# Values times probabilities over four query blocks at once in heads 0 to 6, and the constants at the end of on-chip memory

## The chip, the cores and the metric

The kernel runs on one NeuronCore of a Trainium2 chip. The metric is the device time of one execution in microseconds (us); of several runs the median is taken. The engines are TensorE (PE in the profile, with its weight loads as PEld), VectorE (DVE), ScalarE (ACT), GpSimd (POOL) and SyncE (SP), which only issues transfers here.

## The reference

A two-layer encoder on one sequence of 1024 tokens with 1024 features, all in fp32. Layer 0 mixes tokens by latent attention (A), layer 1 by differential attention (B); both have 8 heads with values 128 wide. Queries go in blocks of 128, and a token sees the chunks of 64 up to its own, so query block i needs keys of blocks 0 to i only.

```python
# mixer A, one query block i
logits = einsum('bqhd,bkhd->bhqk', qn_b, k_nope) + einsum('bqhd,bkd->bhqk', qr_b, k_rope)
logits = where(_chunk_mask(i * Q_BLOCK, s), logits * scale, NEG_BIG)
p = softmax(logits, axis=-1)
o = einsum('bhqk,bkhd->bqhd', p, v)
# mixer B: two maps per head
p = softmax(einsum('bqhmd,bkhmd->bmhqk', q_b, k) * scale - slopes * dist, masked)
a = p[:, 0] - lam * p[:, 1]
o = einsum('bhqk,bkhe->bqhe', a, v)          # then RMSNorm per head
# each layer
x = layernorm(ALPHA * x + mixer(x) @ w_o)
x = layernorm(ALPHA * x + (silu(x @ w_gate) * (x @ w_up)) @ w_down)
```

The change touches the two products of probabilities and values.

## The kernel before, in words

Each matrix product is done in three matmuls on values split into a high part (fp32r) and the low rest: high by high, high by low, low by high. So nearly every operand passes through a copy on ACT that rounds it (the high part) and a subtraction on DVE or GpSimd (the low part).

The program goes in stages: projections of A, attention A, its output projection with layer norm, feed-forward layer 0, attention B, its output projection, feed-forward layer 1. Only the attentions change.

`attention` runs both. It lists blocks (h, i), head by head with query blocks 0 to 7, but the last head in the order 6, 7, 4, 5, 2, 3, 0, 1 (`LAST_ORDER`), because the output projection begins with query blocks 6 and 7. At block b it emits the scores of block b + 2 (`score`), the transposes of block b (`turn`), the work put at that slot by hand (`fill`: the projections of queries, keys and values of the next head, and in B the norms of the head before), and after every second block `mix`, the product with the values for that pair. The order of instructions on each engine is then drawn up by the framework's planner, which simulates the engines with a cost of its own; `tc.high_priority` moves a part ahead in its order (in B the turns by 60 places, in A by 0).

One block: `softmax_block` (L209) computes scores into a PSUM bank, DVE adds the bias and finds the extreme (L222), ACT takes the exponential (L227), and GpSimd and DVE normalise (L1188 in A; L1342 to L1344 in B). `transpose_block` (L234) then turns the block of probabilities, 128 keys at a time, through TensorE (L148) into a PSUM bank of up to four key blocks, and splits them pair of key blocks by pair: the copy on ACT (L250) and the subtraction on DVE (L251) write a tile `[P, 2, 256]`, two key blocks by the 256 queries of a pair of query blocks. `pv_group` (L253) multiplies, for each key block of the pair, values (the weights of the matmul) by these 256 columns, three matmuls each (L262); the last key block of a pair concerns its second query block only, so there the matmuls are 128 wide.

`mix_a` (L1194) copies the 256 columns out of PSUM on ACT (L1198) and stores them with one DMA on SP to `o_dr[0][g][h]`; `mix_b` (L1350) copies them on DVE (L1353) into a tile that holds two heads, and `norm_b` and `norm_b2` norm and store a head later. In A the result takes one of three PSUM banks (`ps_m`) that the projections use too, in B the one bank `o`.

The tiles of transposed probabilities lie in pools `ptp` with five buffers (A) or four (B) for each of high and low. Memory is given out from two ends, left and right. At the very left lies the buffer in which GpSimd's transfers (`nc.gpsimd.dma_start`) put their descriptors; then come the constants (identity for the transposes, ones, small columns). At the right end is a reserved strip, `edge`.

Of the kernel before, what the change touches and what calls it, by code (L numbers as in the profile page):

```python
# [16 lines left out]
P = 128  # L17
# [4 lines left out]
H = 8  # L22
# [20 lines left out]
def trunk(  # L43
# [35 lines left out]
    cp = ctx.enter_context(tc.tile_pool(name="cp", bufs=1))  # L79
    sp = ctx.enter_context(tc.tile_pool(name="sp", bufs=8))  # L80

    ident = cp.tile([P, P], F32, tag="ident", name="ident")
    ones = cp.tile([P, P], F32, tag="ones", name="ones")
    cst = cp.tile([P, 48], F32, tag="cst", name="cst")
    edge = ctx.enter_context(tc.tile_pool(name="edge", bufs=1, side="right"))
    edge.tile([P, 504], F32, tag="edge", name="edge")
# [147 lines left out]
    def transpose_block(ptp, pts, l, i, name):  # L234
        qc = (i % 2) * P
        for jq in range(i // 4 + 1):
            nj = min(4, i + 1 - 4 * jq)
            pt = ps_t(f"pt_{name}_{jq}")
            for jj in range(nj):
                j = 4 * jq + jj  # L240
                tr(pt[:, jj * P:(jj + 1) * P], l[:, j * P:(j + 1) * P])
            for jp in range(2 * jq, 2 * jq + (nj + 1) // 2):
                n = min(2, i + 1 - 2 * jp)
                if i % 2 == 0:
                    pts[jp] = tuple(
                        ptp.tile([P, 2, 256], F32R, tag=f"pt{c}", name=f"pt{c}_{name}_{jp}") for c in "hl"
                    )
                src = pt[:, (jp % 2) * 256:(jp % 2) * 256 + n * P].rearrange("p (j q) -> p j q", j=n)
                hv, lv = (t[:, :n, qc:qc + P] for t in pts[jp])
                ends["pth"] = A.copy(hv, src).ins  # L250
                ends["ptl"] = V.tensor_tensor(lv, src, f32(hv), ALU.subtract).ins  # L251

    def pv_group(pts, g, v_of, name):  # L253
        po = ps_o(f"o_{name}")
        nj = 2 * g + 2
        for j in range(nj):
            hi, lo = pts[j // 2]
            vh, vl = v_of(j)
            c = slice(P, 256) if j == nj - 1 else slice(0, 256)
            first, last = j == 0, j == nj - 1  # L260
            for a, b, st, sp_ in ((vh, hi, first, False), (vh, lo, False, False), (vl, hi, False, last)):
                T.matmul(po[:, c], a, b[:, j % 2, c], start=st, stop=sp_, skip_group_check=True)  # L262
        return po

    def attention(score, turn, mix, fill, la, hp):
# [7 lines left out]
        for b, (h, i) in enumerate(blocks):  # L273
            if b and i % 2 == 0:
                mix(blocks[b - 1][0], blocks[b - 1][1] // 2)
# [7 lines left out]
        mix(blocks[-1][0], blocks[-1][1] // 2)  # L283
# [821 lines left out]
    with ast as st:  # L1105
# [3 lines left out]
        ptp = st.enter_context(tc.tile_pool(name="a1p", bufs=5, side="right", reuse_waits="tile"))  # L1109
# [429 lines left out]
```

## Time and profile before

| | |
|---|---|
| Time, median of 3 runs | 2282.62 us (2281.2 to 2283.95) |
| Time of the profiled execution: span from the first to the last instruction | 2280.9 us |
| PE busy | 2242.7 us (98%), 11410 matmuls |
| DVE, ACT, POOL busy | 1555.2 (68%), 1015.4 (45%), 847.9 us (37%) |
| DMA | 288.28 MB, mean 126 GB/s |
| L262, values times probabilities | 160 matmuls of each of three passes in A, and in B |
| L250 and L251, splitting the transposed blocks | 160 each in A, and in B |
| L1198 (A) and L1353 (B), copying the results out | 32 each |

Busy time counts a matmul from its start to its modelled end, and successive ones overlap: a matmul of 128 by 256 lasts 283 ns in the rows, but the next one starts 0.12 us after it. In rows of the timeline the first number is the start in us from the span's start, the second the length. In grouped rows the count is followed by the busy time, the mean length in ns, and the idle time before them with what ended it.

### The profile page before, as it was taken

How to read it: one execution, taken by the hardware profiler on the slowest of the kernel's cores; microseconds unless marked ns; L12 is line 12 of the kernel's file. 1: busy time of each engine (PE TensorE's matmuls, PEld its weight loads, DVE VectorE, ACT ScalarE, POOL GpSimd, SP SyncE). 2: the span in 40 equal slices, each digit the busy share in tenths (PEclk: the TensorE clock that was granted, in tenths of full speed). 3: DMA queues.
4: the chain of work that ended last, by engine and by line, in shares of the span. 5: the costliest groups of instructions: out<-in, count | busy, mean ns of one | idle time of the engine just before them, and what ended most of it. 6: DMA issues, size and time to landing. Idle time of an engine off the chain costs nothing.

```text
span 2280.9 us, 31110 instructions
## 1 busy us (share of the span) xinstructions
PE 2242.7 (98%) x11410; PEld 1912.7 (84%) x11410; DVE 1555.2 (68%) x2848; ACT 1015.4 (45%) x2097; POOL 847.9 (37%) x676
## 2 busy tenths in 40 slices
PE   8999999999999999999999999999999999999998
PEld 8899998888888887888889898888778888887886
DVE  5676665686766658777576657576677666658778
ACT  4455564342333324445465655564432333324444
POOL 2232341114444445555432424321014444436561
PEclk9999999999999999999999999999999999999999
DMA  5010125334445428544311202054244232337443
GB/s 202 14 35 31 41 71 199 142 132 150 153 149 184 141 102 334 190 175 157 104 45 33 67 27 70 21 211 155 86 164 150 84 114 95 112 128 298 163 178 150
DMA packets 105545, 288.28 MB, mean 126 GB/s; under 512 B 7968, under 2 KB 30112, under 8 KB 94896
## 3 DMA queue, kind: packets, MB, share of 16 engines
q1 hardware_dynamic: 100976, 275.87, 34.1%
q0 software_dynamic: 4416, 10.42, 1.7%
q8 instruction: 90, 1.47, 0.3%
q14 instruction: 63, 0.52, 0.1%
HBM read 205.00 MB, written 77.07 MB: 124 GB/s over the span
## 4 chain that ended last, share of the span: by engine, by line
PE 92%; DVE 3%; DMA 2%; issue 1%; ACT 1%; POOL 0%; SPq 0%; DVEq 0%; POOLq 0%; ACTq 0%
PE gb L549 15%; PE gc L549 10%; PE ga L549 10%; PE dw L830 7%; PE dx L830 5%; PE s_a L219 4%; PE zp_a L417 3%; PE s_b L219 3%; PE dv L830 3%; PE dy L830 3%; PE bp L145 3%; PE bp L143 3%; PE bp L144 3%; PE o_a L262 2%; PE o_b L262 2%; PE hq L1038 1%
## 5 line engine op out<-in xcount | busy, mean ns | idle before, releaser
L503 ACT CAST op_g<-gr 128x512 fp32r<-128x512 f32 x240 | 146.8, 621 | 369.3 <-PE gb L549 180.2
L504 POOL TENSOR_TENSOR op_g<-gr,op_g 128x512 fp32r<-128x512 f32 x104 | 145.2, 1401 | 250.1 <-ACT op_g L503 144.5
L504 DVE TENSOR_TENSOR op_h<-rh,op_h 128x512 fp32r<-128x512 f32 x154 | 158.6, 1057 | 62.1 <-ACT op_h L503 62.1
L549 PE MATMUL ga<-xh_m,op_g 128*128 128x512 f32 x512 | 168.2, 389 | 0.0
L503 ACT CAST op_h<-rh 128x512 fp32r<-128x512 f32 x154 | 92.9, 619 | 138.4 <-PE dx L830 36.5
L830 PE MATMUL dw<-op_w_t,op_h 128*128 128x512 f32 x660 | 151.2, 390 | 0.0
L830 PEld LDWEIGHTS dw<-op_w_t,op_h 128*128 128x128 f32 x660 | 123.6, 188 | 25.7 <-DVE op_h L504 0.2
L227 ACT ACTIVATE l_b<-l_b,mx_b 128x256 f32<-128x256 f32 (+7 forms) x128 | 99.4, 777 | 76.8 <-DVE mx_b L222 72.8
L1343 POOL TENSOR_SCALAR l_b<-l_b,rb,cst 128x128 f32<-128x128 f32 (+3 forms) x64 | 52.5, 821 | 205.1 <-DVE rb L1342 193.6
L830 PE MATMUL dx<-op_w_b,op_h 128*128 128x512 f32 x528 | 123.1, 394 | 5.4 <-ACT op_w_b L503 3.9
L504 POOL TENSOR_TENSOR op_w_t<-tt,op_w_t 128x512 fp32r<-128x512 f32 x66 | 99.4, 1510 | 76.0 <-ACT op_w_t L503 74.7
L830 PEld LDWEIGHTS dx<-op_w_b,op_h 128*128 128x128 f32 x528 | 99.9, 190 | 28.4 <-ACT op_w_b L503 4.7
L504 DVE TENSOR_TENSOR op_g<-gr,op_g 128x512 fp32r<-128x512 f32 x136 | 110.7, 820 | 14.3 <-ACT op_g L503 14.0
L549 PE MATMUL gb<-t4h_f,op_g 128*128 128x512 f32 x352 | 115.9, 390 | 3.3 <-DVE tmp L632 3.3
L504 POOL TENSOR_TENSOR op_g<-s,op_g 128x512 fp32r<-128x512 f32 x40 | 55.5, 1388 | 168.8 <-ACT op_g L503 160.6
L549 PE MATMUL gb<-t3h_f,op_g 128*128 128x512 f32 x352 | 115.5, 389 | 2.0 <-DVE tmp L628 2.0
L549 PE MATMUL gb<-t2h_f,op_g 128*128 128x512 f32 x352 | 115.6, 390 | 0.4 <-DVE op_g L504 0.4
L549 PE MATMUL gc<-t1h_f,op_g 128*128 128x512 f32 x352 | 115.6, 389 | 0.1
L549 PE MATMUL gc<-b22h_f,op_g 128*128 128x512 f32 x352 | 115.3, 389 | 0.0
L549 PEld LDWEIGHTS ga<-xh_m,op_g 128*128 128x128 f32 x512 | 96.1, 188 | 19.9
L143 PE MATMUL bp<-xT_f,h_wb 128*128 128x512 f32 x256 | 101.7, 397 | 0.0
L144 PE MATMUL bp<-xT_f,h_wb 128*128 128x512 f32 x256 | 101.5, 397 | 0.0
(384 smaller groups left out, 6718.9 us busy)
## 6 DMA issues: line engine op xcount, KB each, us to landing
gr<-in_w_gu SPq DMA_DIRECT2D x44, 1024.0 KB, 7.0
rh<-h_dr SPq DMA_DIRECT2D x28, 1024.0 KB, 6.3
h_dr<-sh SPq DMA_DIRECT2D x22, 1024.0 KB, 4.9
h_dr<-hp SPq DMA_DIRECT2D x22, 768.0 KB, 4.1
tt<-in_w_dn SPq DMA_DIRECT2D x22, 512.0 KB, 7.8
rh<-h_dr SPq DMA_DIRECT2D x14, 768.0 KB, 4.3
wo_dr<-op_pwo SPq DMA_DIRECT2D x16, 512.0 KB, 3.5
z<-xs_dr SPq DMA_DIRECT2D x16, 512.0 KB, 10.1
```

The source lines that it names most:

```text
L143: T.matmul(ps_out, lh, rh, start=(i == 0), stop=False)
L144: T.matmul(ps_out, lh, rl, start=False, stop=False)
L145: T.matmul(ps_out, ll, rh, start=False, stop=(i == n - 1))
L219: T.matmul(s[:, :w], lh, rh[:, ks], start=(j == 0), stop=(j == len(q_pass) - 1))
L227: ends["exp"] = A.activation(l[:, :n], l[:, :n], AF.Exp, bias=mx, scale=-1.0, accum_out=sm).ins
L262: T.matmul(po[:, c], a, b[:, j % 2, c], start=st, stop=sp_, skip_group_check=True)
L417: T.matmul(m, a[:, h, :], self.wo[h][w][:, c], start=(start and h == heads[0] and a is oh and w == 0), stop=(stop and h == heads[-1] and a ...
L503: A.copy(hi, src)
L504: return eng.tensor_tensor(lo, src, f32(hi), ALU.subtract).ins
L549: T.matmul(o, w[:, a, kc], x[b][:, k, :], start=(first and k == 0 and (a, b) == (0, 0)), stop=(k == 3 and a == 1), skip_group_check=True,)
L830: T.matmul(o, h[:, a, c], w[:, b_], start=(first and (a, b_) == (0, 0)), stop=(last and a == 1), skip_group_check=True,).ins for a, b_ in ...
L1343: G.tensor_scalar(l1[:, :n], l1[:, :n], r[:, 1:2], nlam, ALU.mult, ALU.mult)
```

## The change

- In heads 0 to 6 of both attentions a mix covers four query blocks instead of two (`wide(h)` is 4); head 7 stays at two. Its matmuls are 512 wide, and 384, 256 and 128 wide for the last three key blocks. A PSUM bank of results holds 512 columns.
- The transposed probabilities lie in tiles of 2048 columns: four key blocks by four query blocks, or for head 7 all eight key blocks by two. One copy and one subtraction split a whole bank of up to four key blocks, in all heads. There are two such tiles for each of high and low.
- `mix_a` copies 512 columns out and issues two DMAs, `mix_b` copies 512 columns.
- The constants move to the right end; `edge` shrinks so that the right end is filled as far as before. The descriptor buffer of GpSimd's transfers shrinks from the default (16384 bytes per partition) to 1024, and a pad keeps the left side at a distance of exactly 16 KB from its old place.

```diff
-    cp = ctx.enter_context(tc.tile_pool(name="cp", bufs=1))
+    cp = ctx.enter_context(tc.tile_pool(name="cp", bufs=1, side="right"))
+    cst = cp.tile([P, 48], F32, tag="cst", name="cst")
+    ones = cp.tile([P, P], F32, tag="ones", name="ones")
+    ident = cp.tile([P, P], F32, tag="ident", name="ident")
+    cp.tile([P, 200], F32, tag="edge", name="edge")
     sp = ctx.enter_context(tc.tile_pool(name="sp", bufs=8))
...
-    edge.tile([P, 504], F32, tag="edge", name="edge")
+    base = ctx.enter_context(tc.tile_pool(name="base", bufs=1))
+    base.tile([P, 48], F32, tag="pad", name="pad")
...
+    def wide(h):
+        return 4 if h < H - 1 else 2
...
-            for jp in range(2 * jq, 2 * jq + (nj + 1) // 2):
-                n = min(2, i + 1 - 2 * jp)
-                if i % 2 == 0:
-                    pts[jp] = tuple(
-                        ptp.tile([P, 2, 256], F32R, tag=f"pt{c}", name=f"pt{c}_{name}_{jp}") for c in "hl"
-                    )
-                src = pt[:, (jp % 2) * 256:(jp % 2) * 256 + n * P].rearrange("p (j q) -> p j q", j=n)
-                hv, lv = (t[:, :n, qc:qc + P] for t in pts[jp])
-                ends["pth"] = A.copy(hv, src).ins
-                ends["ptl"] = V.tensor_tensor(lv, src, f32(hv), ALU.subtract).ins
+            k = jq if n == 4 else 0
+            if k not in pts:
+                pts[k] = tuple(
+                    ptp.tile([P, 2048], F32R, tag=f"pt{c}", name=f"pt{c}_{name}_{jq}") for c in "hl"
+                )
+            src = pt[:, :nj * P].rearrange("p (j q) -> p j q", j=nj)
+            hv, lv = (
+                t.rearrange("p (j c q) -> p j c q", c=n, q=P)[:, 4 * (jq - k):4 * (jq - k) + nj, q]
+                for t in pts[k]
+            )
+            ends["pth"] = A.copy(hv, src).ins
+            ends["ptl"] = V.tensor_tensor(lv, src, f32(hv), ALU.subtract).ins
...
-        nj = 2 * g + 2
+        n = wide(h)
+        nj = n * g + n
         for j in range(nj):
-            hi, lo = pts[j // 2]
+            hi, lo = pts[j // 4 if n == 4 else 0]
             vh, vl = v_of(j)
-            c = slice(P, 256) if j == nj - 1 else slice(0, 256)
+            q0 = max(0, j - n * g) * P
+            at = (j % 4 if n == 4 else j) * n * P
...
-                T.matmul(po[:, c], a, b[:, j % 2, c], start=st, stop=sp_, skip_group_check=True)
+                T.matmul(po[:, q0:n * P], a, b[:, at + q0:at + n * P], start=st, stop=sp_, skip_group_check=True)
...
-            if b and i % 2 == 0:
-                mix(blocks[b - 1][0], blocks[b - 1][1] // 2)
+            if b:
+                hp_, ip = blocks[b - 1]
+                if ip % wide(hp_) == wide(hp_) - 1:
+                    mix(hp_, ip // wide(hp_))
...
-        ptp = st.enter_context(tc.tile_pool(name="a1p", bufs=5, side="right", reuse_waits="tile"))
+        ptp = st.enter_context(tc.tile_pool(name="a1p", bufs=2, side="right", reuse_waits="tile"))
...
-            ob = vp.tile([P, 256], F32, tag="ob", name=f"ob{h}_{g}", bufs=2)
-            A.copy(ob, po[:, :256])
-            nc.sync.dma_start(o_dr[0][g][h], ob)
+            n = wide(h) // 2
+            ob = vp.tile([P, 512], F32, tag="ob", name=f"ob{h}_{g}", bufs=2)[:, :n * 256]
+            A.copy(ob, po[:, :n * 256])
+            for k in range(n):
+                nc.sync.dma_start(o_dr[0][n * g + k][h], ob[:, k * 256:(k + 1) * 256])
...
-        ptp = st.enter_context(tc.tile_pool(name="b1p", bufs=4, reuse_waits="tile"))
+        ptp = st.enter_context(tc.tile_pool(name="b1p", bufs=2, reuse_waits="tile"))
...
-            V.tensor_copy(o_rows(h, g), po[:, :256])
+            n = wide(h) // 2
+            V.tensor_copy(o_rows(h, n * g, n), po[:, :n * 256])
...
-    nc = bacc.Bacc("TRN2", target_bir_lowering=False, num_devices=1)
+    nc = bacc.Bacc("TRN2", target_bir_lowering=False, num_devices=1, dynamic_dma_scratch_size=1024)
```

21 lines of the change are left out of this document (9 added, 12 removed).

## The prediction

> **What bounds the kernel now.** I read the per-core line and the page first, then the chain that ended last, then the two attention stages by stretches, then who made TensorE wait in them, and last the single matmuls in order of time, because the change touches one matmul loop and what feeds it.
>
> ```profile
> core 0: 2280.9 us, clock 0.997
> PE 2242.7 (98%) x11410; PEld 1912.7 (84%) x11410; DVE 1555.2 (68%) x2848; ACT 1015.4 (45%) x2097; POOL 847.9 (37%) x676
> PE 92%; DVE 3%; DMA 2%; issue 1%; ACT 1%; POOL 0%; SPq 0%; DVEq 0%; POOLq 0%; ACTq 0%
> ```
>
> TensorE is busy 98% of the span at full clock and is 92% of the chain. The two attentions lie at about 95 to 355 us (A) and 1130 to 1550 us (B). Stretches of them (columns: stretch, its length, then busy us of PE, its weight loads, DVE, ACT, POOL; granted clock; DMA share; GB/s):
>
> ```profile
> 150.00:200.00 50.00, 50.00 (x338) 46.30 (x337) 33.05 (x99) 29.66 (x81) 16.04 (x18) 1.00 0.12 38
> 250.00:300.00 50.00, 50.00 (x330) 45.91 (x329) 36.09 (x102) 29.10 (x80) 12.65 (x15) 1.00 0.08 25
> 1200.00:1300.00 100.00, 100.00 (x628) 89.52 (x627) 68.52 (x195) 60.26 (x142) 32.95 (x31) 1.00 0.15 43
> 1500.00:1560.00 60.00, 57.65 (x319) 47.70 (x318) 45.16 (x123) 36.04 (x89) 15.42 (x17) 1.00 0.49 189
> ```
>
> TensorE is full in them, VectorE at 66 to 75%, ScalarE at about 60%, GpSimd at about 30%. Only the tail of B (head 7) has gaps. The waits of TensorE confirm it: between 95 and 360 us the view lists none, and between 1130 and 1560 us only these three.
>
> ```profile
> PE zp_a L417 <- DMA wo<-wo_dr: 1.3, 1, 1.3
> PE s_b L219 <- DVE bk L1327: 1.3, 1, 1.3
> PE pt_b L148 <- DVE l_b L1344: 0.8, 2, 0.7
> ```
>
> So inside heads 0 to 6 a microsecond less of TensorE work is a microsecond less of time, as long as no new wait appears, and work saved on ACT or DVE is worth nothing by itself.
>
> **What a matmul costs.** The length of a matmul in the rows overlaps its successor; what counts is the distance from one start to the next. Starts in us, then the modelled length; the last fence is a piece of the chain.
>
> ```profile
> 142.97 0.28 PE L262 MATMUL o_a<-ptl_a,vh 128*128 128x256 f32 x1
> 143.09 0.28 PE L262 MATMUL o_a<-pth_a,vl 128*128 128x256 f32 x1
> 143.21 0.22 PE L262 MATMUL o_a<-pth_a,vh 128*128 128x128 f32 x1
> 143.27 0.28 PE L262 MATMUL o_a<-ptl_a,vh 128*128 128x128 f32 x1
> 143.38 0.27 PE L262 MATMUL o_a<-pth_a,vl 128*128 128x128 f32 x1
> 143.49 0.48 PE L219 MATMUL s_a<-kn,qh 128*128 128x512 f32 x1
> ...
> 158.27 0.34 PE L219 MATMUL s_a<-kn,ql 128*128 128x384 f32 x1
> 158.45 0.34 PE L219 MATMUL s_a<-ck_hi,qr 128*128 128x384 f32 x1
> 158.63 0.27 PE L148 MATMUL pt_a<-ident,l_a 128*128 128x128 f32 x1
> ```
> ```profile
> 226.78 2.81 PE o_a L262 x24
> ...
> 501.78 2.72 PE gb L549 x12
> ```
>
> The three 128-wide matmuls that close a group take 143.49 - 143.21 = 0.28 us together. The 24 of a whole group of pair 3 take 2.81, so its 21 256-wide ones take (2.81 - 0.28) / 21 = 0.1205 each. 512-wide ones with a new weight each take 2.72 / 12 = 0.2267 (the FFN row), 384-wide ones 0.18. Two 256s (0.241) thus cost 0.014 more than one 512: every matmul carries some 13 ns beside its columns, and a 128-wide one does not fall to half of a 256.
>
> **The change, part by part.** (1) The mix over four query blocks. Per head of 0 to 6 and attention the old loop issues, for groups of 2, 4, 6 and 8 key blocks, 3 x (1+3+5+7) = 48 matmuls of 256 and 12 of 128: 48 x 0.1205 + 4 x 0.28 = 5.78 + 1.12 = 6.90 us. The new one has two groups, of 4 and 8 key blocks, in which the last four narrow from 512 to 128: 18 of 512, 6 of 384, 6 of 256, 6 of 128. That is 18 x 0.2267 + 6 x 0.18 + 6 x 0.1205 + 2 x 0.28 = 4.08 + 1.08 + 0.72 + 0.56 = 6.44 us. The columns are the same (4608 x 3); 24 matmuls fewer per head save 0.46 us, and 14 heads save 6.4 us. The 384 row is read to 0.01 us only, which leaves 84 x 0.005 = 0.4 us either way. Head 7 keeps pairs.
>
> On this the Trainium skill says otherwise ("TensorE: Matmul & The Clock Gate", Back-to-back issue gap): columns over 2.4 GHz plus about 2.5 ns for a warm matmul by itself. By that an old head would take 5.91 us and a new one 5.85, and the sum would be 0.8 us instead of 6.4. The rows show about 13 ns where the page has 2.5, with a weight load before every matmul, and 0.28 for three 128s where it gives 0.17; the same section does warn that a stream of loads and matmuls is spaced by both. I take the rows.
>
> (2) Splitting the transposed probabilities: one copy (ACT) and one subtraction (DVE) per bank of up to four key blocks instead of one per pair, in all heads.
>
> ```profile
> L250 ACT CAST pth_a<-pt_a 128x256 fp32r<-128x256 f32 x128 | 45.3, 373 | 25.3 <-PE pt_a L148 14.5 <-DVE ptl_a L251 9.1 <-PE s_a L219 0.4
> L250 ACT CAST pth_a<-pt_a 128x128 fp32r<-128x128 f32 x32 | 8.6, 269 | 7.7 <-DVE ptl_a L251 4.1 <-PE pt_a L148 3.5
> L251 DVE TENSOR_TENSOR ptl_a<-pt_a,pth_a 128x256 fp32r<-128x256 f32 x128 | 51.7, 420 | 13.9 <-ACT pth_a L250 12.7
> L251 DVE TENSOR_TENSOR ptl_a<-pt_a,pth_a 128x128 fp32r<-128x128 f32 x32 | 9.2, 286 | 1.8 <-ACT pth_a L250 1.7
> L1198 ACT COPY ob<-o_a 128x256 f32<-128x256 f32 x32 | 12.0, 375 | 17.9 <-PE o_a L262 10.2 <-issue 6.7 <-DMA o_dr<-ob 0.6
> L1353 DVE COPY bo<-o_b 128x256 f32<-128x256 f32 x32 | 13.5, 421 | 14.0 <-PE o_b L262 13.9
> ```
>
> By the slope from 128 to 256 a 512-wide copy is about 373 + 2 x 104 = 0.58 us on ACT and 420 + 2 x 134 = 0.69 on DVE; the constant is 0.17 and 0.15. A head goes from 20 of each to 12, so 8 x 0.17 = 1.3 us of ACT and 1.2 of DVE go per head, some 20 us of each over 16 heads. Both are covered by a full TensorE: zero. If the cover were gone, they would be a gain. Against them stands a later hand-over: the first matmul of a key quad waits for 0.58 + 0.69 instead of 0.37 + 0.42, about 0.5 us.
>
> (3) The copies out (L1198, L1353) go from four to two per head, each twice as wide; zero on the path by the same cover. The DMAs to o_dr stay 32 and of the same size, issued in twos on SP up to two blocks later; SP has the next head's weights queued behind them, which are asked for a head ahead. Their reader, the output projection, begins with the last head, which is not regrouped. Zero.
>
> (4) Buffers of the transposed probabilities: two wide ones per half (2 x 8 KB) instead of five (A) or four (B) of 2 KB. A second group needs both, so the copy for its second key quad (block 4) waits until the mix over blocks 0 to 3 has read its tile, and the next head's block 0 until the first half of the mix over blocks 4 to 7 is done. Queued behind that copy on ACT are the exponentials of the blocks two ahead, and on them DVE, GpSimd and the next transposes. The new mixes are also longer at a time, 1.9 and 4.6 us. The trace has no such wait, so I bound it: from below zero, since five and four buffers already go round within one head (the last pair takes four) and TensorE shows no wait from it in A; the nearest rows are what the weight loads of the mix wait for now.
>
> ```profile
>   DVE ptl_b L251: 0.4, 1
>   ACT pth_a L250: 0.4, 1
>   DVE ptl_a L251: 0.3, 1
>   ACT pth_b L250: 0.3, 1
> ```
>
> From above it is 0.4 at each of the 28 mixes, 11.2 us. I take zero, since four such waits in 64 mixes is nearer to none, and TensorE has projections and scores of later blocks to run meanwhile.
>
> (5) The identity, ones and small constants at the other end of memory, everything on the left 16 KB lower. No row shows a cost by address: the transposes that read the identity are 0.27 us against scores of every tile. Zero; a nanosecond either way on some 750 transposes bounds it at 0.8 us.
>
> (6) A descriptor buffer of 1 KB instead of the default 16 KB for transfers issued by GpSimd.
>
> ```profile
> q0 software_dynamic: 4416, 10.42, 1.7%
> L1320 POOL DMA_DIRECT2D bq<-bq x32 | 17.7, 553 | 36.1 <-ACT bq L1316 35.8
> bq<-bq POOLq DMA_DIRECT2D x32, 128.0 KB, 2.7
> ```
>
> 4416 packets in all; in B 32 small transfers, landing 2.7 us after issue. If each had to wait for its forerunner to land, GpSimd would stand 32 x 2.7 = 86 us in B with the normalisation of the probabilities queued behind, which is the upper end; the lower is zero, which I take, since the transfers come in twos, several us apart. The Trainium skill ("DMA: Bandwidth & Descriptors", Terms and The descriptor swizzle) gives 16 bytes per descriptor and 9 per engine for a 128-partition transfer; an estimate from it is 64 descriptors, seven transfers at once. No run here shows the limit.
>
> **The sum.** -6.4 + 0. The profiled span is 2280.9, the median of the runs 2282.6, 1.7 us above it; off the median the forecast is 2276.2.
>
> **The rivals.**
> - Stalls at the group edges (slower). Place: the first block of each group, point (4). Break-even is 6.4 / 28 = 0.23 us per mix; at the 0.4 of the wait rows the loss is 11.2 and the time 2282.6 - 6.4 + 11.2 = 2287.4. For it: in B the turns are put 60 places ahead, so the copies run ahead into the buffer wait, and ACT is in order. Against it: TensorE has run 260 us in A without a listed wait at 60% ACT.
> - Half of that, or a TensorE that starves for some microseconds in blocks 4 to 7 because the work of a mix has moved to later blocks: about 2281, no change that can be told.
> - The change doesn't do what it says: the 13 ns belong to the columns and only the page's gap goes. By rows, with 0.2267 / 512 per column for all wide ones and 0.28 for the closing three, 3.1 us go: 2279.5, within the measurement. (By the Trainium skill's gap it would be 0.8 us, 2281.8.)
> - More than the sum: the fewer ACT and DVE instructions also close B's tail, where TensorE is idle 2.35 of 60 us and the three listed waits add to 3.4: 2282.6 - 6.4 - 3.4 = 2272.8.
> - GpSimd's buffer blocks: B stretched by up to 86 us; anything over 6.4 us loses.
>
> **How the numbers follow.** About 0.2% (4.6 us) is what a measurement of this kernel can tell from no change; the runs spread over 2.8 us. Forecast (stalls under 1.8 us in sum) 0.50, more than the sum 0.10: faster 0.60. Half-stalls 0.19, columns only 0.05: same 0.24. Stalls at the edges 0.13, GpSimd's buffer 0.03: slower 0.16. The range runs from 2271 (the tail's gain and a low run) to 2286 (most of the stalls), and leaves out the buffer and the worst stalls. The likeliest case alone is 2274 to 2278.
>
> **What the profile after would show.** L262 with 104 matmuls per pass and attention (7 x 12 + 20) instead of 160, and a chain piece of 24 of them of about 4.6 us; L250 and L251 96 times each per attention; L1198 and L1353 18 times. A's stage some 3.2 us shorter, B's the same, the FFN stages as before. PE waits at ACT or DVE still near none in A: if rows such as o_a behind pth_a, or pt behind l, appear with several us, step (4) was wrong. If L1320 lasts longer than 0.55 us, step (6) was. If starts of 512-wide mix matmuls lie more than 0.227 apart without a wait, step (1) was. What most easily makes the forecast wrong is the order of instructions, which the planner draws up anew for the whole program.

## The result and the profile after

The changed kernel takes 2297.63 us in the median (2296.65 to 2297.93, 5 runs) against 2282.71 (2281.2 to 2283.95, 5 runs) of the kernel before on the same chip: ratio 1.0064, 95% interval 1.0052 to 1.0077. It is 14.9 us slower; the forecast was 2276.2, with a range up to 2286. The profiled execution spans 14.0 us more than before. From its page, the per-core line, the busy times and the shares of the chain:

```profile
core 0: 2294.9 us, clock 0.997
PE 2245.1 (98%) x11074; PEld 1895.9 (83%) x11074; DVE 1543.5 (67%) x2706; ACT 999.3 (44%) x1955; POOL 842.9 (37%) x676
PE 85%; DVE 7%; DMA 3%; issue 2%; ACT 2%; POOL 1%; SPq 0%; DVEq 0%; POOLq 0%; ACTq 0%
```

TensorE issues 336 matmuls fewer and is busy 2.4 us longer in a longer span; its share of the chain that ended last fell from 92 to 85%, and VectorE's rose from 3 to 7. The same stretches as before (columns as there):

```profile
150.00:200.00 50.00, 46.68 (x266) 40.41 (x265) 30.58 (x84) 26.91 (x60) 15.68 (x17) 1.00 0.11 34
250.00:300.00 50.00, 46.34 (x265) 39.58 (x264) 34.24 (x88) 25.89 (x58) 12.55 (x14) 1.00 0.09 27
1200.00:1300.00 100.00, 97.23 (x565) 85.19 (x564) 64.18 (x173) 56.78 (x122) 32.83 (x28) 0.98 0.16 48
1500.00:1560.00 60.00, 56.83 (x312) 48.69 (x311) 46.68 (x114) 35.66 (x77) 13.53 (x16) 0.97 0.58 215
```

In the stretches of A, where TensorE was full, 3.3 and 3.7 of 50 us are now empty, while ACT and DVE have less to do than before. What TensorE waits for, first in A (95 to 370 us), then in B (1120 to 1590 us; total us, times, longest; `s` are scores, `mx` the extreme that L222 finds, `o` the results of a mix, `pth` the high part of the transposed probabilities; line numbers shift by a few from kernel to kernel):

```profile
PE s_a L219 <- DVE mx_a L222: 7.4, 9, 1.9
PE o_a L271 <- ACT pth_a L257: 1.1, 2, 0.9
PE v L143 <- DVE kn L1188: 0.7, 2, 0.4
```
```profile
PE s_b L219 <- DVE bk L1340: 3.2, 2, 2.4
PE s_b L219 <- DVE mx_b L222: 2.2, 3, 1.4
PE pt_b L148 <- DVE l_b L1357: 0.8, 1, 0.8
```

A had no such line before. The largest entry is not at the mix: it is a score matmul (L219) that waits until DVE has emptied a bank of scores (L222). Copies of 512 columns last what was estimated (0.58); these groups, and where A begins and ends (the last numbers of the last two rows are the first and the last start in us):

```profile
L257 ACT CAST pth_a<-pt_a 128x512 fp32r<-128x512 f32 x48 | 27.5, 584 | 13.6 <-PE pt_a L148 13.2
L1210 ACT COPY ob<-o_a 128x512 f32<-128x512 f32 x14 | 8.2, 586 | 15.6 <-PE o_a L271 15.6
L219 PE MATMUL s_a<-kn,qh x192: 220/367/504, 83.8 to 351.3; 128*128 128x384 f32 x48, 128*128 128x512 f32 x48, 128*128 128x320 f32 x32, 128*128 128x448 f32 x32
L271 PE MATMUL o_a<-pth_a,vl x104: 272/336/398, 107.5 to 358.5; 128*128 128x512 f32 x42, 128*128 128x256 f32 x30, 128*128 128x128 f32 x18, 128*128 128x384 f32 x14
```

From the first score to the last matmul of the mix A takes 358.5 - 83.8 = 274.7 us; the same two rows of before give 347.9 - 84.3 = 263.6. Stages measured in this way are what the experiments below are read by (B from its first score to its last mix matmul; the way out of A up to the first matmul of feed-forward layer 0, FFN for short; layer 1 from its first matmul to the last instruction):

| profiled execution, us | A | A's last mix to the FFN | B | FFN layer 1 | span |
|---|---|---|---|---|---|
| before | 263.6 | 93.4 | 418.4 | 654.4 | 2280.9 |
| after | 274.7 | 94.1 | 421.6 | 653.4 | 2294.9 |
| e1_pairs | 265.2 | 94.1 | 429.2 | 652.3 | 2287.9 |
| e2_no_buffer_wait | 274.4 | 100.2 | 426.8 | 651.1 | 2303.6 |
| e3_memory | 264.1 | 93.4 | 418.1 | 653.6 | 2280.5 |
| e5_first_wide / e6_second_wide | 266.7 / 269.6 | 103.5 / 101.9 | 422.6 / 430.6 | 651.6 / 653.1 | 2297.8 / 2307.1 |
| e9_deferred_pairs / e12_tied_pairs | 264.0 / 268.7 | 103.2 / 101.2 | 430.1 / 429.6 | 654.2 / 652.4 | 2297.9 / 2296.9 |
| e14_held_projections | 262.9 | 100.2 | 426.6 | 654.4 | 2295.3 |
| e16_more_out_buffers | 262.9 | 94.5 | 424.3 | 652.2 | 2286.0 |
| e17_wide_in_a | 263.0 | 94.3 | 418.3 | 649.6 | 2278.8 |
| e19_pairs_held | 268.1 | 93.4 | 418.4 | 652.6 | 2284.3 |

Of the 14.0 us, 11.1 are A's and 3.2 B's. From first score to last mix matmul TensorE is empty for 9.7 us of A, 0.2 before. In B, before and after:

```profile
1130.80:1549.16 418.36, 414.75 (x2522) 366.97 (x2521) 286.32 (x803) 248.06 (x576) 135.12 (x129) 1.00 0.22 71
1142.56:1564.17 421.61, 415.16 (x2354) 360.98 (x2353) 276.99 (x725) 242.39 (x515) 134.85 (x130) 0.99 0.23 71
```

TensorE is empty for 3.6 us of B before and 6.5 after. Twice in the changed B, from 1239.0 and from 1515.5 us, its clock is at half for 3.4 us, and TensorE is full in both stretches, so some 3.4 us of work are lost there; in B of before this does not happen. So B has 2.8 us more of empty time, 3.4 us of slow clock and about 3 us less of work, and is 3.2 us longer.

One change of heads in A shows how it comes about. Matmuls of the changed kernel in order of time, then VectorE at the same time (start, length; in brackets idle time and what ended it):

```profile
153.22 0.39 PE L143 MATMUL kn<-ck_hi,h_wa 128*128 128x512 f32 x1
...
153.68 0.40 PE L145 MATMUL kn<-ck_hi,l_wa 128*128 128x512 f32 x1
153.91 0.33 PE L219 MATMUL s_a<-kn,qh 128*128 128x128 f32 x2
...
155.25 0.28 PE L219 MATMUL s_a<-ck_lo,qr 128*128 128x256 f32 x1
157.39 0.62 PE L219 MATMUL s_a<-kn,qh 128*128 128x384 f32 x2 [1.86 <-DVE mx_a L222]
...
160.12 1.15 PE L148 MATMUL pt_a<-ident,l_a 128*128 128x128 f32 x9
...
164.75 0.39 PE L271 MATMUL o_a<-ptl_a,vh 128*128 128x512 f32 x1
164.98 0.40 PE L271 MATMUL o_a<-pth_a,vl 128*128 128x512 f32 x1
```
```profile
153.42 2.79 DVE L1138 TENSOR_TENSOR qrb<-qr,sin 32x512 f32<-32x512 f32 x4
156.43 0.69 DVE L258 TENSOR_TENSOR ptl_a<-pt_a,pth_a 128x512 fp32r<-128x512 f32 x1
157.04 0.28 DVE L222 CUSTOM_DVE_ANT_0 l_a<-s_a,ba 128x128 f32<-128x128 f32 x1
```

The projection of the next head's keys (kn) has its last matmul at 153.68. Then TensorE has only scores of the next head's first blocks left, and a few transposes. They need a bank each, there are two, and DVE, which frees them, is at the rotary part of the queries for 2.79 us. From 155.5 to 157.39 TensorE stands; after the rotary part, DVE first splits a bank of transposed probabilities (0.69 us). The transposes of the old head's block 7 begin at 160.12. Of the mix over blocks 4 to 7 one matmul runs at 162.25 and the others from 164.75, 0.23 us from start to start, as computed. In the kernel before, the mix of blocks 4 and 5 did not depend on block 7, and at the same change of heads it fills the place after the next head's first score. These are the first and the last of its matmuls from 149.96 on:

```profile
149.96 0.34 PE L262 MATMUL o_a<-ptl_a,vh 128*128 128x256 f32 x1
...
152.07 0.28 PE L262 MATMUL o_a<-pth_a,vl 128*128 128x128 f32 x1
```

### The profile page after: what moved, and what is told of

It reads as the page before. It is cut to its first block, busy times and chain, and to the rows that moved or that the text cites. A ratio compares the mean times of both kernels' runs of the same rounds, so it can differ in the third digit from the quotient of the medians.

```text
span 2294.9 us, 30116 instructions
## 1 busy us (share of the span) xinstructions
PE 2245.1 (98%) x11074; PEld 1895.9 (83%) x11074; DVE 1543.5 (67%) x2706; ACT 999.3 (44%) x1955; POOL 842.9 (37%) x676
## 4 chain that ended last, share of the span: by engine, by line
PE 85%; DVE 7%; DMA 3%; issue 2%; ACT 2%; POOL 1%; SPq 0%; DVEq 0%; POOLq 0%; ACTq 0%
PE gb L560 15%; PE gc L560 10%; PE ga L560 10%; PE dw L841 6%; PE zp_a L428 3%; PE s_b L219 3%; PE s_a L219 3%; PE dv L841 3%; PE bp L143 3%; PE bp L144 3%; PE bp L145 3%; PE dy L841 2%; PE o_b L271 2%; PE o_a L271 2%; DVE tt L803 1%
## 5 line engine op out<-in xcount | busy, mean ns | idle before, releaser
L515 POOL TENSOR_TENSOR op_g<-s,op_g 128x512 fp32r<-128x512 f32 x40 | 54.3, 1356 | 166.7 <-ACT op_g L514 110.3
L143 PE MATMUL bp<-xT_f,h_wb 128*128 128x512 f32 x256 | 101.9, 398 | 0.1
L145 PE MATMUL bp<-xT_f,l_wb 128*128 128x512 f32 x256 | 101.4, 396 | 0.0
## 6 DMA issues: line engine op xcount, KB each, us to landing
z<-xs_dr SPq DMA_DIRECT2D x16, 512.0 KB, 10.3
```

Source lines behind the costliest of these rows:

```text
L143: T.matmul(ps_out, lh, rh, start=(i == 0), stop=False)
L145: T.matmul(ps_out, ll, rh, start=False, stop=(i == n - 1))
L515: return eng.tensor_tensor(lo, src, f32(hi), ALU.subtract).ins
```

## The experiments

Five theories stood at the start. *Lumps*: the wide mix has its data only when the last of four blocks is transposed, so TensorE has no independent work at the change of heads. *Buffers*: the copy of transposed probabilities waits on ACT for one of two wide tiles, and the softmax queues behind it (point (4) of the prediction). *Copies*: one copy per bank hands over later. *Memory*: the moved constants or the small descriptor buffer. *Order*: the planner's new order is worse by chance. The code excerpts show only the lines that matter. All times are medians, with the ratio to the kernel before on the same chip and its 95% interval.

**e3_memory: the memory part alone** (attentions as before; constants, pad and 1 KB buffer as after).

```diff
+    cp = ctx.enter_context(tc.tile_pool(name="cp", bufs=1, side="right"))
...
+    nc = bacc.Bacc("TRN2", target_bir_lowering=False, num_devices=1, dynamic_dma_scratch_size=1024)
```

> The kernel before, with only the constants at the right end, the pad, and the descriptor buffer of 1 KB. Theory memory: 2290 or more. Theories buffers, lumps, order: 2281 to 2284, the stages as before to 0.5 us, and GpSimd's transfers still issued in 0.55 us.

2281.91 us, 0.9997 (0.9988 to 1.0007). No stage moves by more than 0.8 us. The queries' small transfers on GpSimd take as long as before (553 ns there), with a landing time of 3.0 us (2.9 before in the same stretch, 1120 to 1560 us):

```profile
L1320 POOL DMA_DIRECT2D bq<-bq x32 | 17.7, 555 | 36.6 <-ACT bq L1316 36.0 <-issue 0.5
bq<-bq POOLq DMA_DIRECT2D x30, 128.0 KB, 3.0
```

*Memory* falls.

**e1_pairs: pairs in all heads, the rest as after.**

```diff
     def wide(h):
-        return 4 if h < H - 1 else 2
+        return 2
```

> The changed kernel, but with the mix over two query blocks in all heads again; the constants' place, the small descriptor buffer, the single copy per bank and the two 8 KB tiles stay. Theory buffers (two tiles make the copies on ACT wait for the mix) and theory lumps (TensorE lacks the mix of the first pair as reserve work in blocks 4 to 7): both are gone with pairs, so the time is that of before, 2281 to 2284 us, attention A again 264 us from its first score to the first output projection matmul instead of 275. Theory memory (places or the descriptor buffer): stays near 2297. Theory order (the planner's new order is bad by chance): anywhere from 2278 to 2300, A and B moving independently.

2289.96 us, 1.0038 (1.0023 to 1.0052). A is back at 265.2: of the 11.1 us, 9.5 come and go with the wide mix, and 1.6 stay with e1. The time misses the 2281 to 2284 because of B: 429.2, with its loss at the end (head 7), where TensorE waits 4.1 us at once for a normalised block. Part of that figure is a shifted border. In e1 21 matmuls of the output projection, which came after the last mix, run before it, and the way from B to feed-forward layer 1 is 4.8 us shorter (72.6 instead of 77.4; 70.8 to 71.4 in e9, e11 and e12 below). Both together are 501.8 us in e1, 495.7 in the kernel before.

**e2_no_buffer_wait: a third tile for the probabilities in A** (13 instead of 16 blocks of columns in the tile that holds the triangle; one `ob` buffer pays for it).

```diff
+                d = tri and (jq == i // 4 if n == 4 else i // 2 in (1, 2))
-                    ptp.tile([P, 2048], F32R, tag=f"pt{c}", name=f"pt{c}_{name}_{jq}") for c in "hl"
+                    ptp.tile([P, (13 if d else 16) * P], F32R, tag=f"pt{c}{'d' if d else ''}",
+                             name=f"pt{c}_{name}_{jq}", bufs=(2 if d else 1) if tri else 2) for c in "hl"
...
-            ob = vp.tile([P, 512], F32, tag="ob", name=f"ob{h}_{g}", bufs=2)[:, :n * 256]
+            ob = vp.tile([P, 512], F32, tag="ob", name=f"ob{h}_{g}", bufs=1)[:, :n * 256]
```

> The changed kernel, but in A the tiles of transposed probabilities no longer wait for a mix: two tiles of 13 blocks for the diagonal quads and one of 16 for the full quad, for each of high and low; one buffer instead of two for the copied result pays for it. B as changed. Theory buffers: the ACT waits for the mix (12.0 us in five in A) go, and A falls from 275 to 261 to 264 us, the time to 2283 to 2287. Theory lumps: the waits at ACT go, A stays over 270, the time over 2292. Theory order: A anywhere, with other places of waiting.

2306.3 us, 1.0106 (1.0091 to 1.0121). Of the 8.7 us that its span has over the changed kernel's, 6.2 lie in the way out of A, where copies into the single `ob` wait 5.4 us for stores, and 5.2 in B, whose instructions are the same. The wait it is aimed at is there in the changed kernel, in ACT's waits from 95 to 362 us:

```profile
ACT pth_a L257 <- PE o_a L271: 12.0, 5, 3.6
```

In e2 ACT has no such wait in A any more, yet A takes 274.4 and TensorE waits for mx_a 7.7 us. In A, *buffers* names a real wait that isn't on the path. For B no run takes it away (9.6 us in eight waits in the changed kernel).

**e5_first_wide and e6_second_wide: only blocks 0 to 3, or only 4 to 7, in one mix.**

```diff
-    def wide(h):
-        return 4 if h < H - 1 else 2
+    def span(h, i):
+        return (0, 4) if h < H - 1 and i < 4 else (i - i % 2, 2)      # e5
+        return (4, 4) if h < H - 1 and i > 3 else (i - i % 2, 2)      # e6
```

> The changed kernel with the four-block mix only for query blocks 0 to 3 of heads 0 to 6; blocks 4 to 7 go in pairs, so that the mix of blocks 4 and 5 (2 us of TensorE) is there to run while blocks 6 and 7 are on their way. Theory lumps: A comes back to 262 to 266 us, nearly all of the 11 lost. Theory order: A has no reason to differ from the changed kernel's 275, or lands anywhere.

> The reverse: the four-block mix only for blocks 4 to 7, pairs for blocks 0 to 3. Theory lumps: the loss stays, A 270 to 276 us, TensorE waiting for score banks around the change of heads. Theory order: anywhere.

2298.89 us, 1.0069 (1.0054 to 1.0084), and 2312.55, 1.0131 (1.0115 to 1.0146). A takes 266.7 and 269.6: 1.5 and 4.4 over e1, both together 9.5. Each lies just outside what *lumps* asked for, 262 to 266 and 270 to 276. The mix over blocks 4 to 7 carries more, and TensorE's waits for score banks are none in e5 and 4.4 us in e6. In both, the way out of A is longer too: TensorE waits 7.5 and 6.4 us at once for the last copy into `ob` (7.8 and 6.1 in e9 and e12 below), which lies on ACT behind copies of the output projection's input that wait for their transfer.

**e4_rope, e7_later_projections, e8_three_ahead: more work near the gap by the order of the program.** e4 puts the rotary part of the queries two slots earlier, e7 the projections of the second half one slot later, e8 scores three blocks ahead with three banks (and one bank less for the transposes).

```diff
-                at(b + 7, q_rope, h // 2, 1)
+                at(b + 5, q_rope, h // 2, 1)                          # e4
-            at(b + (6 if h < H - 1 else 4), q_nope, h, 1)
-            at(b + (7 if h < H - 1 else 5), k_nope, h, 1)
+            at(b + (7 if h < H - 1 else 4), q_nope, h, 1)             # e7
+            at(b + (8 if h < H - 1 else 5), k_nope, h, 1)
-PS_BUFS_A = (2, 3, 3)
+PS_BUFS_A = (3, 3, 2)                                                 # e8
...
-        attention(score_a, turn_a, mix_a, fill, 2, (0, 0))
+        attention(score_a, turn_a, mix_a, fill, 3, (0, 0))            # e8
```

> The changed kernel, with the second half of the rotary queries (five DVE operations in a row, 3.5 us) put two slots earlier, from block 7 to block 5 of the head before. Theory lumps: the two places where TensorE waits 2.0 + 0.5 + 0.3 us for a score bank while DVE works on them go, A falls by 4 to 8 us, the time to 2290 to 2294. Theory buffers: the same waits for the mix stay and A stays at 273 to 276, the time at 2296 to 2298. Theory order: A anywhere.

> The changed kernel with the second halves of the query and key projections in A (2.0 and 1.4 us of TensorE) one slot later, in block 7 and in block 0 of the next head instead of blocks 6 and 7, so that TensorE has independent work at the change of heads. Theory lumps: the waits for score banks there fall by half or more, A to 263 to 270. Theory order: A 271 to 278 with other places of waiting.

> The changed kernel with the scores of A three blocks ahead instead of two, three score banks instead of two (two instead of three for the transposes) and five tiles of probabilities instead of four; the first and the last head's key projections a slot earlier, as the scores need them. Theory lumps: TensorE can run the next head's first scores while block 7 is on its way, the waits for score banks (7.4 us in nine) go, A 260 to 268. If the score banks are only where a shortage elsewhere shows (DVE), A stays over 270.

2303.12 us, 1.0092 (1.0077 to 1.0107); 2302.85, 1.0095 (1.0079 to 1.011); 2314.39, 1.0134 (1.0117 to 1.0151). A stays at 274.9, 275.5 and 277.3, and *lumps* misses all three. In e4 the rotary part no longer stands in the gaps (the one at the change of heads shown is 1.36 us instead of 1.86), but the waits for score banks still sum to 7.7 us. In e8 they fall to 1.5, and TensorE is empty elsewhere instead, 10.5 us of A in all against 9.7. So neither the rotary part on DVE nor the number of score banks is the cause by itself. The place in the program decides little, since the planner draws up its own order.

**e10_reserve: the mix over blocks 0 to 3 emitted after block 6.**

```diff
+                if late and wide(hp_) == 4:
+                    if ip in (6, 7):
+                        mix(hp_, ip - 6)
```

> The changed kernel with the tiles of the run e2_no_buffer_wait in A, the results copied out 256 columns at a time from two buffers as before, and in A, heads 0 to 6, the mix of blocks 0 to 3 held back to block 7 (1.9 us of TensorE kept for the change of heads). Theory lumps: the waits there shrink by up to 1.9 us a head, A from 274.5 to 262 to 270. Otherwise A stays at 273 to 277. With the two buffers the output projection of A is back at 93 to 95 us.

2293.23 us, 1.0046 (1.0031 to 1.0061); A 272.8. The expected 270 is missed; a small part of the way, again by a place in the program alone.

**e9_deferred_pairs and e12_tied_pairs: pairs, but in lumps.** e9 emits the two pairs of a half together, though their data are ready as early as before; e12 also ties the first of them to the transposes of the half's last block (an added dependency), which is what the wide mix has to wait for. Both have tiles of their own for each pair, so that no buffer waits.

```diff
+                if st and tied[0]:                                    # e12 only, in pv_group
+                    behind(m.ins, tied[0])                            # e12 only
...
+                    elif ip % 4 == 3:
+                        tied[0] = ends["tr"]                          # e12 only
+                        mix(hp_, ip // 2 - 1)
+                        tied[0] = None                                # e12 only
+                        mix(hp_, ip // 2)
```

> Pairs in all heads as in the run e1_pairs, but in A, heads 0 to 6, the mixes of two pairs are emitted together after the second, with their own tiles so that no buffer waits; TensorE's work is that of pairs (261 us by the spacing of its matmuls), and only the moment is that of four blocks. Theory lumps (the mix of the first pair is missing as work in between): A rises from 265 to 271 to 279. If the wide matmuls, the buffers or a chance order are the cause: A stays at 263 to 268.

> The run e9_deferred_pairs, but the mix of the first pair of each four blocks in A is also tied on TensorE behind the transposes of the fourth block, as the wide mix is by its data (in e9 it was only put later in the program, and the planner could still pull it forward). Matmuls stay 256 wide. Theory lumps, in the form that the moment at which the data is complete is what counts: A rises from 264 to 270 to 278, with TensorE waiting for score banks as in the changed kernel. If the width or the planner's order is the cause: A stays at 263 to 267.

2299.13 us, 1.0068 (1.0051 to 1.0085), and 2300.17, 1.0078 (1.0062 to 1.0093). A is 264.0 in e9 and 268.7 in e12. So the place in the program does nothing here, and the time at which the data are complete costs 4.7 us with no wide matmul at all. e12 fell short of the 270 it should have reached at least: TensorE is empty for 3.9 us of A, not for 9.7, and waits for score banks at two places only. Why it stops there isn't shown.

**e14_held_projections: the changed kernel, with work kept for the gap.** Query and key projections of the next head's second half (3.4 us a head) are tied to come after the transposes of block 6.

```diff
+            if i == 0 and after:
+                behind(m.ins, after)
...
             transpose_block(ptp, pts.setdefault((h, i // wide(h)), {}), lt.pop((h, i)), h, i, f"a{h}_{i}")
+            if i == 6 and h < H - 2:
+                held[h + 1, 1] = ends["tr"]
...
-                    for k in range(NQ)])
+                    for k in range(NQ)], held.get((h, hf)))
```

> The changed kernel with the second halves of the query and key projections of heads 1 to 6 in A (3.4 us of TensorE a head) tied behind the transposes of block 6 of the head before, so that they are there to run while block 7 is on its way. Theory lumps: the waits for score banks shrink, A from 274.7 to 260 to 269. Otherwise A 272 to 280, since the new ties can only cost.

2295.45 us, 1.0058 (1.0043 to 1.0073). A falls from 274.7 to 262.9. The same change of heads, TensorE:

```profile
153.00 0.34 PE L220 MATMUL s_a<-ck_lo,qr 128*128 128x384 f32 x1
153.17 1.03 PE L152 MATMUL pt_a<-ident,l_a 128*128 128x128 f32 x8
153.96 0.47 PE L143 MATMUL kn<-c,h_wa 128*128 128x512 f32 x1
...
155.19 0.39 PE L147 MATMUL kn<-ck_hi,l_wa 128*128 128x512 f32 x1
...
155.45 0.71 PE L220 MATMUL s_a<-kn,qh 128*128 128x512 f32 x2
```

The key projection (kn) now lies between the scores, and the scores find their banks free: with e1, e2 and e12, *lumps* is shown for A, in the form that the data of the wide mix come late and too little else is left to do. But the way from A to the feed-forward layer grew by 6 us. Waits of TensorE and of ACT from 330 to 365 us in e14 (`zp_a` is the output projection's result), and a stretch of that time (columns as before):

```profile
PE zp_a L143 <- ACT ob L1215: 5.0, 1, 5.0
```
```profile
ACT ob L1215 <- DMA o_dr<-ob: 3.2, 1, 3.2
```
```profile
348.50:355.30 6.80, 3.55 (x8) 2.81 (x9) 1.16 (x2) 1.51 (x3) 2.32 (x2) 0.50 0.91 302
```

The output projection's bank is freed by the last copy into `ob`, which waits until the transfer of an earlier one has read its buffer. From within that wait on, TensorE's clock is at half for 6.8 us, and 3.55 us of work run in them.

**e16_more_out_buffers: e14 with four `ob` buffers.**

```diff
-            ob = vp.tile([P, 512], F32, tag="ob", name=f"ob{h}_{g}", bufs=2)[:, :n * 256]
+            ob = vp.tile([P, 512], F32, tag="ob", name=f"ob{h}_{g}", bufs=4)[:, :n * 256]
```

> The kernel of e14 (projections held back in attention A), with four instead of two buffers for the copied-out result `ob` of A. In e14 A itself took 262.9 us but the way from its last mix to the feed-forward layer took 100.2 us where the kernel before takes 93.4, with 5.0 us of TensorE waiting for a PSUM bank that the copy into `ob` frees, itself waiting for a store. If that wait is the cause, the way is back at 93 to 95 us, A stays at 262 to 264, and the time falls by about 6 us from e14, to about 2289. If the longer way comes from the order drawn up anew, it stays at 99 to 103 us and the time at about 2295. B is expected at 418 to 430 us by either.

2289.39 us, 1.0033 (1.002 to 1.0046), as expected: the way out is 94.5 and the wait 0.7.

```profile
PE zp_a L143 <- ACT ob L1215: 0.7, 1, 0.7
```

**B: e11_last_head_fine, e15_redraw, e17_wide_in_a, e18_held_in_b.** e11 is e1 with copies by pairs in head 7; e15 is the kernel before with B's transposes put 50 places ahead instead of 60; e17 is e16 with B's code as before; e18 is e16 with B's second key projection (5.4 us a head) held like A's.

```diff
+            step = 2 if h == H - 1 else 4                                             # e11
-        attention(score_b, turn_b, mix_b, fill, 2, (0, 60))
+        attention(score_b, turn_b, mix_b, fill, 2, (0, 50))                           # e15
+        attention(score_b, turn_b, mix_b, fill, 2, (0, 60), lambda h: 2)              # e17
+                held[h + 1, 1, 1] = ends["tr"]                                        # e18, in turn_b
```

> The run e1_pairs (pairs everywhere, single copies per bank) with the copies and subtractions of head 7 again per pair of key blocks. Theory copies (the wider hand-over of 0.5 us is what lengthens the end of B, where the last head stands alone): B falls from 429 to 417 to 421, the time to 2276 to 2283. Theory order: B's end lands anywhere between 415 and 432.

> The kernel before with the transposes of B put 50 places ahead instead of 60: the same work, another order. Theory order for the end of B (between 47 and 58 us from the last head's transposes on, by the run, for the same instructions): B moves by 2 us or more either way and A not at all. If B stays within 1 us of 418.4, its end is not that sensitive and the single copies or the tiles of head 7 have to be its cause.

> The kernel of e16, with attention B as in the kernel before: pairs of query blocks, one copy and one subtraction per pair, four buffers. A alone is wide. Theory lumps with reserve: A 262 to 264 us, its way out 93 to 95, so up to the start of B at most 1 us more than before. If the loss in B comes from the wide mix and the wide hand-over there, B is back at 418 to 422 us and the time 2280 to 2286. If it comes from the order being drawn up anew whenever A changes, whatever B's instructions are, B takes 424 to 430 and the time is 2287 to 2293.

> The kernel of e16, and in attention B the projection of the second half of the next head's keys (24 matmuls, 5.4 us per head) is held behind the transposes of query block 6 of heads 0 to 5, as work kept for the time in which the wide mix waits for block 7. Theory lumps: TensorE's waits at the changes of heads in B go, as in A, and heads 0 to 6 of B take 370 to 373 us instead of 376 in the changed kernel; with the end of B as in e14 (about 51 us) B is 421 to 424. If B's loss has nothing to do with reserve, B stays at 426 or becomes longer.

e11: 2287.31 us, 1.002 (1.0011 to 1.0029), B 428.7. With the way to feed-forward layer 1 it is 499.6, against 501.8 in e1 and 495.7 in the kernel before: the size of the copies in head 7 is at most 2.2 of e1's 6.1 us. e15: 2285.58, 1.0013 (1.0003 to 1.0022): one number of the planner alone makes B 422.5, and A 263.7. e17: 2278.79, 0.9982 (0.9973 to 0.9991), below the expected 2280 to 2286; B is 418.3. e18: 2297.71, 1.0067 (1.0052 to 1.0082); B becomes 435.8, with TensorE empty for 13.9 us and at half clock for 20.5. At a change of heads in e18 a score waits for the split of a key projection:

```profile
1329.15 0.33 PE L220 MATMUL s_b<-bk,bq 128*128 128x128 f32 x1 [1.59 <-DVE bk L1345]
```

B's old code takes 418.1 to 418.4 in before, e3, e17 and e19, whatever A is. The wide B has the same instructions in after, e2, e4, e7, e8, e10, e14 and e16, where only A differs, and takes 421.6 to 428.3. What differs is empty time (6.4 to 10.3 us) and time at half clock (6.8 to 15.8 us). An estimate: less the empty time and half of the time at half clock, B is 410.1 to 412.0 us in these eight kernels and in e18, and 413.8 to 416.2 in before, e3, e15, e17 and e19. So the wide form does save work in B too, and loses more by waits and by the slow clock, in an order that is sensitive to everything ahead of it. Which of its parts (width, two tiles, copy per bank) brings the waits isn't settled; holding back work, which mends A, makes B worse in the one form that was tried.

**e19_pairs_held: e17 with pairs in A,** to measure the wide mix by itself.

```diff
     def wide(h):
-        return 4 if h < H - 1 else 2
+        return 2
```

> The kernel of e17 (attention A wide, projections held back, four `ob` buffers, attention B as before) with one difference: A's mixes go back to pairs of query blocks. Hand-over, held projections and buffers stay. It measures what the wide mix itself is worth once TensorE does not wait for it: e17's A is 263.0 us. If the prediction's 0.46 us per head is right, A here is 3.2 us longer, 266; if only a page's gap of a few ns per matmul goes, 0.4 us longer, 263.4; if wide mixes still cost more in waits than they save, A is shorter than 263. For the whole time the same, about 2282, 2279 or below 2278, as far as the order of the feed-forward layers stays; it is redrawn too, and has come out between 649 and 654 us for layer 1 in these runs, so the stage decides.

2285.0 us, 1.001 (1.0 to 1.0019). First and last starts in A of e17, then of e19:

```profile
L220 PE MATMUL s_a<-kn,qh x192: 220/340/497, 85.8 to 341.4; 128*128 128x384 f32 x48, 128*128 128x512 f32 x48, 128*128 128x320 f32 x32, 128*128 128x448 f32 x32
L272 PE MATMUL o_a<-pth_a,vl x104: 272/334/401, 109.6 to 348.8; 128*128 128x512 f32 x42, 128*128 128x256 f32 x30, 128*128 128x128 f32 x18, 128*128 128x384 f32 x14
```
```profile
L220 PE MATMUL s_a<-kn,qh x192: 220/360/499, 84.9 to 346.1; 128*128 128x384 f32 x48, 128*128 128x512 f32 x48, 128*128 128x320 f32 x32, 128*128 128x448 f32 x32
L272 PE MATMUL o_a<-pth_a,vl x160: 272/282/287, 100.6 to 353.0; 128*128 128x256 f32 x128, 128*128 128x128 f32 x32
```

A is 263.0 wide and 268.1 in pairs, more than the 266 expected: under these ties the wide mix is worth 5.1 us. TensorE's waits in A are 0.9 us longer in e19. The mix's own matmuls, added up from each start to the next matmul's start without waits, take 57.4 us in e19 and 53.7 in e17, 3.7 less; the rest is other matmuls in another order. The ties also cost pairs something: A is 265.2 in e1, which is in pairs without them.

## Why the prediction was wrong, point by point

- **The reading of the bound.** "A microsecond less of TensorE work is a microsecond less of time, as long as no new wait appears": the saving came (next points), the condition did not hold. The step that failed is the zero that the sum has for waits, with its reason in point (4), "TensorE has projections and scores of later blocks to run meanwhile". At the changes of heads it had not: TensorE is empty for 9.7 us of A instead of 0.2, mostly at scores that wait for a bank. The listing without a wait in A was taken as room, when small mixes stood where little else was left to run. The change made the work slightly smaller and moved it in time.
- **The rival that named it** ("a TensorE that starves for some microseconds in blocks 4 to 7 because the work of a mix has moved to later blocks") had the mechanism and the place, but was priced at about half of the 6.4 us, for a result of 2281. In A alone the wide mix cost 9.5 us net against e1, and TensorE is busy 8.6 us less in the 250 us from 100 to 350, where it had 249.92 before:

```profile
sum 250.00, PE 241.34 PEld 210.92 DVE 157.52 ACT 137.39 POOL 79.81; mean PE 48.27 PEld 42.18 DVE 31.50 ACT 27.48 POOL 15.96
```

- **(1) The wide mix's saving**, forecast as 3.2 us in each attention, was right in kind and a little low. By the starts of its matmuls without waits, the mix takes 57.8 us in A before and 54.1 after, and 58.0 and 54.3 in B: 3.7 us each, in the changed kernel itself. The sum for the columns alone, 1.55 us in each, falls short. So does the estimate of 0.4 us by the gap of the Trainium skill ("TensorE: Matmul & The Clock Gate", Back-to-back issue gap). Starts of 512-wide mix matmuls lie 0.23 us apart in the rows above.
- **(2) The wider hand-over at zero.** A is 1.6 us longer in e1, which has the single copies and the two tiles but no wide mix. It is 264.0 in e11, which copies by pairs in head 7 alone, and in e9, which has the single copies and tiles of its own; so what costs the 1.6 isn't shown.
- **(3) Copies out at zero** holds in the changed kernel (0.7 us more on the way out). In e14, where A ends earlier, the two `ob` buffers cost 6 us (against e16).
- **(4) Buffers at zero.** The wait exists, 12.0 us on ACT in A, but taking it away leaves A as it is (e2). So zero was right for A, and is untested for B. The sign named for this step, o_a behind pth_a, came with 1.1 us; the 7.4 us stood at s_a behind mx_a, which the prediction did not name. The slower rival, built on it, came nearest in time (2287.4) for a wrong reason.
- **(5) and (6) at zero** were right (e3).
- **The warning about the order**, at the end of the prediction, had no price. It deserved one: B, forecast 3.2 us shorter, is 3.2 longer in the changed kernel and up to 9.9 longer in variants with the same instructions in B. The slow clock after waits, some 3.4 us in the changed B, had no term at all.

**A version that beats the kernel before** is e17, wide in A with held projections and four `ob` buffers: 2278.79 us, ratio 0.9982 (0.9973 to 0.9991). The gain cannot be put down to the wide mix. A is 0.6 us shorter than before, but up to the end of B the profiled execution is 2.7 us later, and feed-forward layer 1 is 4.8 shorter, whose code is untouched and which came out between 648.8 and 654.4 us in these kernels. Against its twin with pairs, e19, it is 6.2 us faster, of which 5.1 lie in A.

## What to carry to other kernels

Regrouping work into fewer, larger pieces saves the fixed cost per instruction, but it also makes data complete later: before pricing it, look in the timeline for what the bound engine will do at the places where the small pieces used to stand. If that is nothing, work must be kept for it, with a dependency and not with a place in the program (e12 and e14 against e7, e9 and e10); here this took back the loss of 11 us in A (263.0 in e17, 263.6 before), and not more. A stage whose list of waits is empty is not one with room: put a price on its order.

## What the runs showed of the hardware

In these traces TensorE's clock falls to half after some waits of a few microseconds, in the attentions and the ways out of them for 3.4, 6.8 or 10.2 us at a time. Stretches of the changed kernel in B (the number ahead of the DMA share is the granted clock), and TensorE's rows in them:

```profile
1234.00:1239.00 5.00, 2.23 (x13) 1.41 (x13) 4.09 (x14) 3.15 (x10) 1.64 (x2) 1.00 0.00 0
1239.00:1242.40 3.40, 3.40 (x13) 2.81 (x12) 2.67 (x10) 2.86 (x8) 0.55 (x1) 0.50 0.00 0
1242.40:1246.00 3.60, 3.60 (x19) 3.01 (x18) 3.03 (x11) 2.92 (x9) 1.05 (x2) 1.00 0.00 0
```
```profile
1235.75 0.38 PE L219 MATMUL s_b<-bk,bq 128*128 128x256 f32 x1 [1.42 <-DVE mx_b L222]
...
1241.21 0.63 PE L219 MATMUL s_b<-bk,bq 128*128 128x512 f32 x1
1241.64 0.63 PE L219 MATMUL s_b<-bk,ql 128*128 128x512 f32 x1
```

Between 1234 and 1239 TensorE is busy for 2.23 of 5 us, and its longest gap is 1.42 us; then it runs 3.4 us at half speed, in which 512-wide matmuls start 0.43 us apart, and loses 1.7 us more. The Trainium skill ("TensorE: Matmul & The Clock Gate", HAM oscillation) puts the rule as no idle gap over about 3.4 us. Here shorter gaps close together were enough, so a wait of a few microseconds can cost more than its length.
